# Six buffers in place of three for the tiles named `lt` in a hybrid attention and RWKV-7 decoder layer

## The chip, the cores and the metric

The kernel runs on one core of a Trainium2 chip. The metric is the device time of one execution in microseconds. A core has five engines that work side by side, each through its own instructions in a fixed order, and wait for each other by semaphores: PE (matmuls, and transposes done as matmuls), DVE (vector work), ACT (activations and copies), POOL (elementwise work and fills) and SP (here it only issues DMAs). PEld in a profile is PE's loading of weights.

## The reference, cut to what matters

One decoder layer on a sequence of 1024 tokens of width 1024: a dilated window attention and an RWKV-7 time mixing side by side, merged by gates, and then a squared-ReLU MLP. The change lies in the RWKV-7 part, which is a recurrence over the tokens for 16 heads of 64 channels:

```python
def step(state, inp):
    r_t, w_t, k_t, v_t, a_t, b_t = inp
    sa = jnp.einsum('bhvk,bhk->bhv', state, a_t)
    state = (state * w_t[:, :, None, :] + sa[..., None] * b_t[:, :, None, :]
             + v_t[..., None] * k_t[:, :, None, :])
    return state, jnp.einsum('bhvk,bhk->bhv', state, r_t)
...
y = wkv7_scan(rh, wh, kh, vh, -kk, kk * ah)
mu = jnp.mean(y, axis=-1, keepdims=True)
var = jnp.mean(jnp.square(y - mu), axis=-1, keepdims=True)
y = ((y - mu) * lax.rsqrt(var + GN_EPS)).reshape(B, S, C) * gn_w + gn_b
```

## The kernel before, in words

The heads are handled in 8 pairs (m = 0 to 7; the text calls them pair 0 to pair 7), since two heads fill the 128 partitions. The tokens are cut into 16 chunks of 64, and inside a chunk the recurrence becomes a triangular system. For each pair these steps are written down, in the order of the string `ORDER` (a letter for the step, a digit for the pair):

- P and G: projections, which are dense matmuls on PE at L307 (G are the 16 gate projections, of which one is written per pair and the rest at the end). They need nothing of the recurrence and fill PE between the steps below.
- E and F: the small projections and the features of the pair (L694 to L709 on DVE). L709 writes the second operand of the next step, in two halves.
- g: the products inside the chunks (PE L749), which DVE takes out of PSUM with a mask (L755 into `lm`, L757 into `fe`).
- I, the inverse: DVE L769 transposes `lm` into `lb`; 30 dependent steps of two instructions (L775, L777) on DVE solve the unit triangular systems with `lb` and a scratch area in `tt`; L781 transposes the result into `tt`. From L769 to the end of L781 is called the solve below. PE transposes further operands meanwhile (L785, L722).
- L, the local part: block-diagonal operands `bd` are filled by copies (`place`, L805), from `tt` for the first and the third of them. PE transposes parts of `lm` (L816) and `ar` (L820) into PSUM, ACT copies these into two tiles `xx` (L817, L822). Then come six groups of four matmuls (L838), each of a `bd` with an `xx`, their results (L840, L843, L845), and 8 groups of four matmuls (L853) that finish `fe` (L854, L855, L858).
- C, the chain: 16 dependent steps over the chunks, in each a matmul of each head (PE L874) and its scaling (DVE L877). ACT copies the result into `y` (L880).
- N, the norm: squares of `y` into `sq` (L888), their sum (DVE L890), a reciprocal root in small DVE instructions (L137 to L142), its product with `y` (POOL L894), transposes on PE (L900), ACT L904, POOL L908, DVE L912, and a DMA out of `sq`.

The tiles are given out from pools, and a scheduler, when the kernel is built, sets the fixed order of each engine's instructions: it takes the written order as priority, and an instruction gets its place once its operands and a free buffer are there by the scheduler's own reckoning. So the number of buffers decides both which tile an instruction waits for on the chip, and where it stands in its engine's queue. Matmul results go to PSUM tiles named `s`, of which there are two buffers.

Six tiles of 4 KB per partition are taken under the one name `lt` for each pair, in this order:

```python
lb = f4.tile([64, 32, 32], F32, name="lt", bufs=NLT)
tt = f4.tile([64, 32, 32], F32, name="lt", bufs=NLT)
xx = [f4.tile([128, 2, 4, 128], F32, name="lt", bufs=NLT) for h in range(2)]
y = f4.tile([128, 16, 64], F32, name="lt", bufs=NLT)
sq = f4.tile([128, 16, 64], F32, name="lt", bufs=NLT)
```

With three buffers in turn, `lb` and the second `xx` share one, `tt` and `y` share one, and the first `xx` and `sq` share one. So L817 into the second `xx` waits until L781 has read `lb`.

Of the kernel before, what the change touches and what calls it, by code (L numbers as in the profile page):

```python
# [30 lines left out]
OGR = ((0, 1), (2, 3), (4,), (5,), (6,), (7,))  # L31
OPV = 0
OQ = 0
NBD, NFT, NLT, NW, NGT, NRK = 5, 6, 3, 4, 2, 4
NGA, NAD = 1, 7
NAP, NSA = 4, 3
DVE_K, PE_K, POOL_S, NAT, NX0 = (0, 2, 3, 5), (1, 4, 6, 7), (1, 3), 6, 4
# [1374 lines left out]
```

## Time and profile before

| | us |
|---|---|
| median of three runs (2270.26 to 2278.08) | 2275.87 |
| the profiled execution, its own time | 2280.91 |
| span of that execution, first to last instruction | 2279.2 |
| PE busy in the span (10002 instructions) | 2090.6 (92%) |
| DVE busy | 1567.8 (69%) |
| ACT busy | 1036.3 (45%) |
| POOL busy | 621.9 (27%) |

Busy time is the time in which an engine had an instruction of the program running. PE's matmuls overlap, so that a busy PE is not PE at its peak. The granted clock of PE is either full (1.00) or half (0.50) at any time; its mean over this execution is 0.961. The solves of the eight pairs run from 503 us to 1279 us of the span, one about every 106 us.

### The profile page before, as it was taken

What the parts mean: (1) busy time and instruction counts of PE and PEld (TensorE: products, weight loads), DVE (VectorE), ACT (ScalarE), POOL (GpSimd) and SP (SyncE); (2) the same over time, 40 slices, a digit from 0 to 9 for tenths busy, and PEclk for the clock granted to TensorE, in tenths of its full rate; (3) what the DMA queues carried; (4) which work ended last, traced back from release to release, by engine and by line L of the source; (5) the groups of instructions that cost most, each with busy time, mean ns of one, the idle gap of its engine ahead of it and who ended that gap; (6) DMA issues with size and microseconds to landing.
All of it is one profiled execution on the core that took longest, in us unless ns stands there. A gap on an engine that the chain in (4) does not pass through costs nothing. (4 is left out here: it accounts for less than half of the span.)

```text
span 2279.2 us, 28241 instructions
## 1 busy us (share of the span) xinstructions
PE 2090.6 (92%) x10002; PEld 1628.6 (71%) x10002; DVE 1567.8 (69%) x2845; ACT 1036.3 (45%) x2018; POOL 621.9 (27%) x461
## 2 busy tenths in 40 slices
PE   6798999988989989898989999998699999999997
PEld 3676676666777767677777778876467777788876
DVE  5845555468879787867877744428766553799997
ACT  5534433345454635444645442126545443533332
POOL 2504310321213131222222133201000000988860
PEclk9999999999999999998998999999899999999998
DMA  7513311100011110101010164323354333433222
GB/s 257 169 31 102 98 38 33 56 28 24 25 33 37 31 34 29 34 29 34 24 48 31 54 202 144 125 93 118 118 168 161 116 106 125 155 128 114 93 102 74
DMA packets 156315, 194.88 MB, mean 86 GB/s; under 512 B 10729, under 2 KB 110211, under 8 KB 154127
## 3 DMA queue, kind: packets, MB, share of 16 engines
q1 hardware_dynamic: 156175, 193.08, 25.5%
q8 instruction: 79, 1.29, 0.2%
q14 instruction: 61, 0.50, 0.1%
HBM read 152.14 MB, written 40.90 MB: 85 GB/s over the span
## 5 line engine op out<-in xcount | busy, mean ns | idle before, releaser
L307 PE MATMUL d<-hh,w_h 128*128 128x512 f32 x960 | 329.0, 415 | 7.2 <-ACT w_h L64 4.0
L307 PE MATMUL d<-hl,w_h 128*128 128x512 f32 x960 | 331.1, 415 | 2.9 <-DVE hl L280 2.9
L307 PE MATMUL d<-hh,w_l 128*128 128x512 f32 x960 | 324.8, 410 | 2.6 <-DVE w_l L65 2.6
L1108 PE MATMUL m<-op 128*128 128x512 f32 x1272 | 295.8, 394 | 11.5 <-POOL op L65 6.4
L65 POOL TENSOR_TENSOR w_l<-w_t,w_h 128x256 fp32r<-128x256 f32 x160 | 129.3, 810 | 633.6 <-PE d L307 293.4
L1108 PEld LDWEIGHTS m<-op 128*128 128x128 f32 x1272 | 240.0, 190 | 66.9 <-POOL op L65 10.6
L1108 PE MATMUL m<-big,op 128*128 128x512 f32 x1152 | 275.1, 399 | 5.1 <-ACT op L64 2.1
L1108 PEld LDWEIGHTS m<-big,op 128*128 128x128 f32 x1152 | 212.8, 188 | 67.3 <-DVE u L1220 4.2
L64 ACT CAST w_h<-w_t 128x256 fp32r<-128x256 f32 x272 | 108.7, 404 | 316.4 <-PE d L307 230.7
L307 PEld LDWEIGHTS d<-hl,w_h 128*128 128x128 f32 x960 | 181.5, 193 | 45.5 <-issue 10.1
L307 PEld LDWEIGHTS d<-hh,w_h 128*128 128x128 f32 x960 | 180.8, 193 | 46.3 <-issue 5.7
L307 PEld LDWEIGHTS d<-hh,w_l 128*128 128x128 f32 x960 | 181.1, 192 | 44.0 <-issue 8.5
L64 ACT CAST op<-t 128x512 fp32r<-128x512 f32 (+1 forms) x152 | 114.2, 776 | 182.8 <-PE m L1108 121.5
L65 DVE TENSOR_TENSOR op<-t,op 128x512 fp32r<-128x512 f32 (+1 forms) x124 | 118.5, 975 | 28.0 <-ACT op L64 27.8
L153 POOL TENSOR_TENSOR macc<-macc,ada_t 128x512 f32<-128x512 f32 x56 | 87.5, 1564 | 181.3 <-ACT macc L151 162.7
L1266 POOL TENSOR_TENSOR t<-big 128x1024 f32<-128x1024 f32 x7 | 16.9, 2410 | 352.1 <-DMA big<-in_w_ff_dram 331.3
L1282 DVE TENSOR_TENSOR big<-big,m 128x1024 f32<-128x1024 f32 x88 | 104.4, 1210 | 3.8 <-PE m L1108 3.8
L775 DVE TENSOR_TENSOR lt<-lt 64x30 f32<-64x30 f32 (+14 forms) x240 | 96.9, 404 | 8.2
L777 DVE TENSOR_TENSOR lt<-lt 64x30 f32<-64x30 f32 (+14 forms) x240 | 94.2, 392 | 7.7
L874 PEld LDWEIGHTS ch<-sv,fe 128*128 128x128 f32 x512 | 83.3, 191 | 20.3 <-DVE sv L877 8.9
L65 DVE TENSOR_TENSOR w_l<-w_t,w_h 128x256 fp32r<-128x256 f32 x112 | 61.6, 555 | 48.6 <-ACT w_h L64 34.9
L65 POOL TENSOR_TENSOR op<-t,op 128x1024 fp32r<-128x1024 f32 x28 | 93.2, 3339 | 4.3 <-ACT op L64 4.3
(379 smaller groups left out, 3925.8 us busy)
## 6 DMA issues: line engine op xcount, KB each, us to landing
w_t<-in_w_in_dram SPq DMA_DIRECT2D x240, 128.0 KB
ada_t<-in_ada_w_dram SPq DMA_DIRECT2D x64, 256.0 KB
fS<-ft SPq DMA_DIRECT2D x64, 256.0 KB
t<-in_w_ff_dram SPq DMA_DIRECT2D x16, 1024.0 KB
big<-fS SPq DMA_DIRECT2D x16, 1024.0 KB
big<-in_w_ff_dram SPq DMA_DIRECT2D x16, 1024.0 KB
x<-in_x_dram SPq DMA_DIRECT2D x16, 512.0 KB
ada_t<-in_ada_w_dram SPq DMA_DIRECT2D x16, 512.0 KB
```

The costliest lines, as they stand in the source:

```text
L64: nc.scalar.copy(hi, t)
L65: (eng or nc.vector).tensor_tensor(lo, t, hi.bitcast(F32), OP.subtract)
L153: nc.gpsimd.tensor_tensor(acc, acc, t, OP.add)
L307: nc.tensor.matmul(p[:, 512 * half + cs.start:512 * half + cs.stop], a, b[half][k][:, cs], start=k == ks[0] and i == 0, stop=k == ks[-1] a ...
L775: nc.vector.tensor_tensor(q, lb[:, s + 1:32, s:s + 1].to_broadcast([64, n, s]), lb[:, s:s + 1, 0:s].to_broadcast([64, n, s]), OP.mult)
L777: nc.vector.tensor_tensor(lb[:, s + 1:32, 0:s], lb[:, s + 1:32, 0:s], q, OP.add)
L874: nc.tensor.matmul(ps[h][:, c8, :], fe[b][:, h, c8, :], sv[h][b][:, c8, :], start=True, stop=True)
L1108: self.nc.tensor.matmul(p, s, m, start=start and k == 0 and i == 0, stop=k == len(a) - 1 and i == 2, skip_group_check=not start)
L1266: vb.tensor_tensor(sb[:, 0], wr[:, k1, h2], wr[:, k1, h1], OP.subtract)
L1282: nc.vector.tensor_tensor(acc[nm][h], acc[nm][h], ps2[h], OP.add)
```

## The change

One constant becomes 6, so that each of the six tiles of a pair has a buffer of its own, which it shares only with the tile of the same role of the next pair:

```diff
-NBD, NFT, NLT, NW, NGT, NRK = 5, 6, 3, 4, 2, 4
+NBD, NFT, NLT, NW, NGT, NRK = 5, 6, 6, 4, 2, 4
```

No instruction is added or removed. The order of the instructions changes from the local part of pair 0 to the start of the merge; ahead of that and behind it it is the same. Three places follow.

On PE, between the end of pair 3's early transposes and its first L838, before the change (`b_6579` is `lm` of pair 3; `bd_3719` and `bd_3717` are the first operands of its two heads; rows of L307 are left out at the cut):

```order
L816 MATMUL s<-ident,b_6579 128x128 x4
L307 MATMUL d<-hh,w_h 128x512
L816 MATMUL s<-ident,b_6579 128x128 x4
L820 MATMUL s<-ident,ar 128x128 x4
...
L307 MATMUL d<-hh,w_l 128x512 x2
L816 MATMUL s<-ident,b_6579 128x128 x8
L820 MATMUL s<-ident,ar 128x128 x4
L838 MATMUL s<-lt,bd_3719 128x128 x4
L307 MATMUL d<-hh,w_h 128x512 x2
L838 MATMUL s<-lt,bd_3717 128x128 x4
```

The same place in the changed kernel:

```order
L816 MATMUL s<-ident,b_6579 128x128 x4
L820 MATMUL s<-ident,ar 128x128 x4
L816 MATMUL s<-ident,b_6579 128x128 x4
L307 MATMUL d<-hl,w_h 128x512 x2
L816 MATMUL s<-ident,b_6579 128x128 x4
L820 MATMUL s<-ident,ar 128x128 x4
...
L307 MATMUL d<-hh,w_l 128x512
L838 MATMUL s<-lt,bd_3719 128x128 x4
L838 MATMUL s<-lt,bd_3717 128x128 x4
```

The second eight L816 and four L820 have moved from behind the long run of L307 to ahead of it, and L838 is now the first instruction of pair 3 behind that run. It is so in pairs 1 to 7, where the run itself has between 68 and 85 L307 in place of 74 to 88; in pair 0 all sixteen L816 stay behind the run, as before. In pairs 5 and 7, seven of the eight groups of L853 stand ahead of the chain's first L874, where four did before.

On DVE, at the end of pair 3's chain and the start of its norm, which pair 4's products (L755 and L757, `b_7453` is `lm` of pair 4) are woven into, before the change (`b_7360` is an operand of pair 4 that the features write):

```order
L705 TENSOR_TENSOR b_7360<-rkv,ft 128x8x64
L877 TENSOR_SCALAR sv<-ch_7292,dd 64x64
L877 TENSOR_SCALAR sv<-ch_7291,dd 64x64
L707 COPY dd<-ft 64x8 x2
L708 TENSOR_TENSOR ar<-ft 128x2x256
L877 TENSOR_SCALAR sv<-ch_7292,dd 64x64
L709 TENSOR_TENSOR ar<-rkv,ft 128x2x256
L755 TENSOR_TENSOR b_7453<-s,gmask 128x4x2x32
L757 TENSOR_TENSOR fe<-s,gmask 128x4x64
L755 TENSOR_TENSOR b_7453<-s,gmask 128x4x2x32
L757 TENSOR_TENSOR fe<-s,gmask 128x4x64
L890 TENSOR_REDUCE va<-lt 128x16
```

The same place in the changed kernel:

```order
L877 TENSOR_SCALAR sv<-ch_7292,dd 64x64
L704 SCALAR_TENSOR_TENSOR b_7360<-ft 128x8x64
L705 TENSOR_TENSOR b_7360<-rkv,ft 128x8x64
L707 COPY dd<-ft 64x8 x2
L708 TENSOR_TENSOR ar<-ft 128x2x256
L709 TENSOR_TENSOR ar<-rkv,ft 128x2x256
L890 TENSOR_REDUCE va<-lt 128x16
L755 TENSOR_TENSOR b_7453<-s,gmask 128x4x2x32
L891 TENSOR_SCALAR va<-va 128x16
L757 TENSOR_TENSOR fe<-s,gmask 128x4x64
L137 TENSOR_SCALAR rsg_r<-va 128x16
L755 TENSOR_TENSOR b_7453<-s,gmask 128x4x2x32
```

The last L877 of the chain now stands ahead of five feature instructions that stood among the chain's steps, and the first two pairs of L755 and L757 have moved behind L890. Pair 6 has the same order as pair 4, and pair 2 nearly the same. Before the change, pairs 3, 5 and 7 already had L890 ahead of all their L755, and still do.

On PE, at the same point: pair 4's last products, and pair 3's transposes of the norm (`b_7360` as above), before the change:

```order
L749 MATMUL s<-ar,b_7360 128x128 x8
L307 MATMUL d<-hl,w_h 128x512
L785 MATMUL s<-ident,b_7360 128x128 x4
L307 MATMUL d<-hl,w_h 128x512
L900 MATMUL ch_7427<-ident,lt 128x128 x4
L900 MATMUL ch_7436<-ident,lt 128x128 x4
```

The same place in the changed kernel:

```order
L749 MATMUL s<-ar,b_7360 128x128 x8
L307 MATMUL d<-hh,w_h 128x512
L749 MATMUL s<-ar,b_7360 128x128 x5
L900 MATMUL ch_7427<-ident,lt 128x128 x4
L900 MATMUL ch_7436<-ident,lt 128x128 x4
L749 MATMUL s<-ar,b_7360 128x128 x3
L785 MATMUL s<-ident,b_7360 128x128 x4
```

Pair 4's last products now stand behind the norm's transposes of pair 3. It is so for pairs 2, 4 and 6; for pairs 3, 5 and 7 it was so before the change and is so after it.

## Rows read from the trace of the kernel before

**Rows 1.** Windows view, solve's end to next solve's start: engines' busy time, PEclk, DMA, GB/s.
```profile
538.50:605.90 67.40, 64.32 (x353) 52.68 (x353) 49.28 (x121) 35.23 (x69) 10.73 (x12) 0.86 0.05 15
645.70:705.30 59.60, 56.38 (x349) 46.58 (x350) 47.41 (x119) 34.42 (x64) 10.90 (x14) 0.97 0.08 25
742.60:816.20 73.60, 68.75 (x385) 55.69 (x385) 52.03 (x122) 37.01 (x67) 14.70 (x17) 0.91 0.09 28
854.10:915.30 61.20, 58.09 (x356) 47.39 (x356) 48.35 (x120) 34.73 (x65) 11.62 (x15) 0.97 0.09 27
953.80:1031.80 78.00, 73.42 (x386) 60.18 (x387) 51.59 (x122) 38.51 (x71) 14.88 (x17) 0.85 0.09 26
1069.90:1131.80 61.90, 58.90 (x356) 48.67 (x356) 48.23 (x118) 34.88 (x65) 11.50 (x15) 0.95 0.08 26
1169.60:1243.00 73.40, 68.89 (x381) 56.90 (x381) 50.54 (x121) 38.15 (x72) 14.18 (x16) 0.87 0.10 33
```

**Rows 2.** Waits of PE from 490 to 1345 us: total, times, longest.
```profile
PE s L816 <- ACT lt L817: 37.6, 8, 6.2
```

**Rows 3.** Timeline of PE behind pair 3's solve: start, duration, idle before it.
```profile
854.65 1.97 PE L816 MATMUL s<-ident,b 128*128 128x128 f32 x8 [5.24 <-ACT lt L817]
...
857.26 1.22 PE L838 MATMUL s<-lt,bd 128*128 128x128 f32 x8
```

**Rows 4.** Timeline of DVE at the same place.
```profile
850.31 3.83 DVE L781 STREAM_TRANSPOSE lt<-lt 32x1024 f32<-32x1024 f32 x2
854.16 1.82 DVE L805 COPY bd<-lt 32x128 f32<-32x128 f32 x6
858.51 0.45 DVE L805 COPY bd<-lt 32x128 f32<-32x128 f32 x2 [2.53 <-PE s L838]
```

**Rows 5.** Timeline of PE behind pair 4's solve, at half clock.
```profile
957.38 1.91 PE L838 MATMUL s<-lt,bd 128*128 128x128 f32 x8
```

**Rows 6.** Timeline of DVE ahead of pair 4's solve.
```profile
903.44 0.29 DVE L877 TENSOR_SCALAR sv<-ch,dd 64x64 f32<-64x64 f32 x1
...
915.26 4.00 DVE L769 STREAM_TRANSPOSE lt<-b 32x1024 f32<-32x1024 f32 x2
```

**Rows 7.** Timeline of DVE ahead of pair 3's solve.
```profile
790.42 0.55 DVE L877 TENSOR_SCALAR sv<-ch,dd 64x64 f32<-64x64 f32 x2
...
796.20 0.35 DVE L707 COPY dd<-ft 64x8 f32<-64x8 f32 x2
...
798.97 1.21 DVE L890 TENSOR_REDUCE va<-lt 128x16 f32<-128x1024 f32 x1
...
816.16 1.97 DVE L769 STREAM_TRANSPOSE lt<-b 32x1024 f32<-32x1024 f32 x1
```

**Rows 8.** Timeline of PE in that stretch.
```profile
797.78 0.62 PE L307 MATMUL d<-hl,w_h 128*128 128x512 f32 x2
798.24 0.61 PE L307 MATMUL d<-hh,w_l 128*128 128x512 f32 x2
...
801.59 1.13 PE L749 MATMUL s<-ar,b 64*128 64x128 f32 x8 [2.51 <-DVE fe L757]
```

**Rows 9.** Windows view: pair 3's chain, then tails ahead of pairs 4, 3, 5.
```profile
874.70:904.20 29.50, 28.68 (x180) 23.38 (x179) 26.98 (x67) 15.70 (x26) 4.54 (x6) 1.00 0.06 15
903.40:915.30 11.90, 11.56 (x77) 9.25 (x75) 10.74 (x34) 4.48 (x9) 5.61 (x6) 1.00 0.08 23
790.40:816.20 25.80, 22.34 (x121) 17.57 (x119) 19.33 (x46) 7.69 (x13) 9.63 (x10) 0.87 0.07 21
1001.00:1031.80 30.80, 27.33 (x123) 21.81 (x123) 19.84 (x46) 8.89 (x16) 10.11 (x10) 0.72 0.06 18
```

**Rows 10.** Timeline in pair 4's solve: POOL's last sum of the norm and DVE.
```profile
921.81 2.51 POOL L908 TENSOR_TENSOR lt<-lt,rkv 128x1024 f32<-128x1024 f32 x1 [5.48 <-ACT lt L904]
922.13 2.36 DVE L775 TENSOR_TENSOR lt<-lt 64x150 f32<-64x150 f32 x1
```

**Rows 11.** Timeline of PE in pair 1's local part: one group of L853 at full clock.
```profile
665.50 1.05 PE L853 MATMUL s<-fe,b 128*128 128x128 f32 x8
```

## The prediction

> **What bounds the kernel now.** I read the page first: PE is busy 92% of the span, and the change touches only the RWKV-7 part, about 490 to 1340 us. There I split the time by pairs with the windows view. A solve keeps DVE busy and takes about 38 us, as from the L769 at 816.16 to the end of L781 at 854.14 [rows 4, 7]. The change adds nothing to it. What differs is the stretch from one solve's end to the next one's start: 59.6, 61.2 and 61.9 us ahead of pairs 2, 4 and 6, but 73.6, 78.0 and 73.4 us ahead of pairs 3, 5 and 7 [rows 1]. In these stretches no engine is alone the bound: PE is busy for 56 to 73 us of them and DVE for 47 to 52, and they hand results to each other. So the reader should see a loop over the pairs (solve, local part, chain, products of the next pair, solve), in which a step that comes earlier brings all later steps forward. PE's projections (L307) fill its gaps in that loop; since the changed order leaves only 7 more of them behind the last solve, I count the time of the loop, not PE's work, which stays the same.
>
> Then I read PE's waits. The largest is in front of L816: 37.6 us in 8 waits, one for each pair [rows 2]. The timeline shows its cause: in pair 3 PE is idle for 5.24 us, until L817 can write the second `xx`, which is free only when L781 has read `lb` [rows 3, 4]. After that come eight L816 (1.97 us), four L820, and L838 at 857.26, which is 3.1 us after the solve's end at 854.14.
>
> **The change part by part.** No instruction comes or goes; buffers and order change.
>
> *The wait at L816.* With a buffer of its own, `xx` is filled before the solve ends, and PE meets the solve only at L838, whose `bd` is copied from `tt`. DVE's six copies took 1.82 us, 0.30 each [rows 4]; two of them belong to the first head, so L838 can start some 0.7 us behind the solve instead of 3.1: 2.4 us earlier. In pairs 0, 4 and 6 the first L838 came 3.6 us behind, as in pair 4, where it stands at 957.38 [rows 5] and the solve ended at 953.8 [rows 1]: 2.9 us. Five times 2.4 and three times 2.9 make 20.7 us. DVE gains with it, since its L805 waited 2.53 us for that L838 [rows 4]. The wait itself doesn't go: PE still runs out of projections before the solve ends, and the moved transposes cover only a part. So the granted clock, which is at the lower of its two levels (1.2 GHz in place of 2.4) behind this wait, will now be low under L838: eight of them took 1.91 us at half clock [rows 5] and 1.22 us where the clock recovered under them [rows 3]. I take 0.7 us off for each pair, 5.5 in all. This term is a gain of 15.2 us, between 13.7 (only 2.4 in each pair, and the 0.7 lost) and 20.7 (nothing lost).
>
> *The rule that promises more.* The Trainium skill's page "Perfetto Trace Analysis", section "Optimization Strategy", says that the same gap coming back on the engine that should be busy can mean that there are too few buffers for the next tile. By it the gap would close, and the sum for this term would be 37.6 us. The trace agrees on the cause, L817's wait for the buffer [rows 2], but not on the price, since L838 needs the same solve.
>
> *The tails ahead of pairs 2, 4 and 6.* Here the changed order speaks against the change. Before, the last chain step of pair 3 (L877) ended at 903.73 on DVE and the solve of pair 4 began at 915.26, 11.5 us later [rows 6]. Pair 3's own tail was of the other kind: from the last L877, which ended at 790.97, to L769 at 816.16 it took 25.2 us [rows 7], since DVE first finished the features, then took L890, and only then cleared PSUM with L755 and L757, while PE stood idle for 2.51 us [rows 8] and then ran at a low clock (0.87 of full in the mean, 0.72 ahead of pair 5 [rows 9]). In the changed order pairs 2, 4 and 6 get that kind. Their tail is then: L704, L705, L707, L708 and L709, 2.8 us (796.20 to 798.97), and from L890 to L769 17.2 us (798.97 to 816.16) [rows 7]: 20.0 us, so 8.5 us more than 11.5. Three things lessen it. The features that moved leave the chain shorter by up to 2.8 us if DVE sets the chain's pace, and by nothing if PE does; pair 3's chain had PE busy 28.7 of 29.5 us and DVE 27.0 [rows 9], nearly alike, and I take 1.9. The norm now comes ahead of the solve by more, so POOL's L908 may lie less beside the solve's instructions, of which one took 2.36 us next to it [rows 10], against about 0.3 for its neighbours: 0 to 2.0, I take 1. And PE's wait ahead of the second L749 is shorter here: 19 projections stand ahead of it behind the chain, 4.4 us at 0.23 us each (797.78 to 798.24 for two [rows 8]), against 2.8 us of features and the 2.6 us from L890 to the second L749 (798.97 to 801.59) [rows 7, 8], so it is about 1.0 us in place of 2.51. The low clock in the tail ahead of pair 3 cost 3.4 us (a mean of 0.87 over 25.8 us is 6.7 us at half speed, of which half is lost); I take half of it away, 1.7. That leaves 8.5 - 1.9 - 1.0 - 1.7 = 3.9 us for each, 11.7 us for the three. The bounds for one are 0.3 us (8.5 - 2.8 - 2.0 - 3.4) and 13.5 us (8.5 and the 5.0 by which the tail ahead of pair 5 was longer than that ahead of pair 3 [rows 9]).
>
> *The clock, by the skill.* The Trainium skill's page "TensorE: Matmul & The Clock Gate", section "HAM oscillation — how this bites in real kernels", says that a wait which returns in each round of a loop makes the clock fall anew each time, and that half of the throttled time is lost. The 3.4 us above are worked out in that way; rows 9 show the fallen clock in two of the three tails that have the wait and a full one where it is missing.
>
> *The chains of pairs 4 and 6.* In the local parts that follow the solves of pairs 5 and 7, and by the same order in both, three more groups of L853 stand ahead of the first L874. At 1.05 us for a group [rows 11] this delays a chain by 0 (they had to run anyway) to 3.2 us; I take 1 for each, 2 in all.
>
> *The tails ahead of pairs 3, 5 and 7* keep their order: 0, or a gain of up to 5.0 if the one ahead of pair 5 takes the shorter time of pair 3's. The first stretch hardly changes in order. The bonus, the DMA out of `sq` and the start of the merge lie beside PE's projections and cost nothing; without that cover the bonus alone would be L908's 2.5 us [rows 10]. The 7 projections left for the end cost 1.6 us at 0.23 each.
>
> **The sum**: -15.2 + 11.7 + 2 + 1.6 = +0.1 us. The profiled execution took 2280.9 us, so 2281.0; it is 5.0 us over the median of the runs shown, so 2276 us as a median. That is no change: a measurement of this kernel tells about 0.3%, 6.8 us, from nothing.
>
> **The rivals.** *Slower, the tails decide*: the low clock stays in all three new tails and nothing is given back in the chain, so 8.5 to 11 us for each, 25 to 33 in all, with 2 to 6 for the chains of pairs 4 and 6 and 1.6 for the end, against 15: +14 to +26, about 2293. For it: the wait of 2.51 us and a low clock behind it came with each of the tails of that kind: the stretches ahead of pairs 3, 5 and 7 have a mean clock of 0.85 to 0.91, the others but the first 0.95 to 0.97 [rows 1]. It decides from about 6 us for each tail. Against it: PE's wait there is shorter. *Faster, the order of the tails costs little*: DVE sets the pace of the chain and the clock holds, so about 1 us for each tail, and most of the gain of 15 to 20 us stays: about -13 us, 2263. For it: the same work is done, only later, and the longest tail (pair 5) can hardly get worse. *The gap closes*, as the page on traces has it: -37.6 + 11.7 + 3.6, about 2254. Against it stands L838's need of `tt`. That the change doesn't do what it says I leave out, since the moved L816 show that the buffers are free.
>
> **Chances.** No change (within 0.3%) 0.38; slower by the tails 0.31; faster 0.31, of which 0.04 for the closed gap. The likeliest case alone would lie between 2269 and 2283. The range leaves out the closed gap and the ends where all bounds fall together: 16 us below 2276 to 20 us above it, 2260 to 2296.
>
> **What would show it.** Right: PE's wait at L816 is gone, and a wait of about 3 to 4 us stands at L838 in each pair, with L838 some 0.7 us behind the end of L781; DVE's wait ahead of the second L805 is gone; the stretches ahead of pairs 2, 4 and 6 are 2 us longer than before and those ahead of 3, 5 and 7 some 2 us shorter. Wrong: all stretches shrink (faster), or those ahead of pairs 2, 4 and 6 take over 68 us with a granted clock below 0.9 (slower), or the first L838 is held by something else than L805.

## The result, and the profile after

The changed kernel takes 2301.3 us (2290.6 to 2306.8, median of 4 runs) beside 2275.9 us (2270.3 to 2278.1) of the kernel before on the same chip: a ratio of 1.011 with a 95% interval of 1.0068 to 1.0151. It is 25 us slower, and 5 us outside the predicted range. Its profiled execution took 2299.8 us, with a span of 2298.0 us and a mean granted clock of 0.954, where the kernel before had 0.961. Two of the kernels below each had one execution with a mean granted clock under 0.7 (2740 and 2868 us), which is left out of their medians.

The windows view from one solve's end to the next one's start, which answers to [rows 1]:

```profile
538.20:602.70 64.50, 59.76 (x345) 48.53 (x346) 50.23 (x119) 33.08 (x61) 10.16 (x11) 0.92 0.05 13
642.40:712.30 69.90, 65.34 (x353) 52.37 (x353) 49.12 (x119) 33.57 (x59) 13.38 (x16) 0.89 0.08 24
748.50:825.20 76.70, 71.16 (x373) 57.72 (x373) 52.02 (x122) 35.00 (x62) 14.71 (x17) 0.86 0.09 27
863.60:931.50 67.90, 62.90 (x358) 50.62 (x359) 50.53 (x121) 33.68 (x60) 13.10 (x15) 0.93 0.09 26
967.90:1040.90 73.00, 67.57 (x376) 53.42 (x377) 51.67 (x122) 34.74 (x62) 15.11 (x17) 0.93 0.09 28
1079.00:1150.50 71.50, 66.01 (x353) 53.54 (x353) 50.16 (x119) 34.52 (x61) 12.89 (x15) 0.86 0.07 23
1186.70:1261.30 74.60, 70.35 (x373) 56.64 (x373) 50.68 (x121) 35.55 (x65) 14.41 (x16) 0.87 0.10 33
```

Ahead of pairs 2, 4 and 6 the stretch grew by 10.3, 6.7 and 9.6 us, to 69.9, 67.9 and 71.5. The other four changed by -2.9, +3.1, -5.0 and +1.2 us. The seven make +23.0 us; the solves became 2.6 us shorter in sum. Pair 7's solve ends at 1298.8 us in place of 1278.7, and behind that nothing more is lost: the whole loss arises in the loop over the pairs.

PE's waits from 490 to 1365 us (total, times, longest), to be set beside [rows 2]:

```profile
PE s L838 <- ACT bd L805: 19.8, 4, 5.5
PE s L838 <- DVE bd L805: 16.2, 3, 6.0
PE s L749 <- DVE fe L757: 10.6, 8, 2.6
```

The wait at L816 is gone, and 36.0 us in place of its 37.6 stand at L838, as forecast, though 5.1 us in each of seven pairs where the forecast had 3 to 4. The timelines of PE and of DVE behind pair 3's solve answer to [rows 3] and [rows 4], and the last row is the chain's last L877, which answers to the first of [rows 6]:

```profile
864.21 3.75 PE L838 MATMUL s<-lt,bd 128*128 128x128 f32 x16 [5.14 <-ACT bd L805]
```
```profile
859.76 3.81 DVE L781 STREAM_TRANSPOSE lt<-lt 32x1024 f32<-32x1024 f32 x2
863.60 1.42 DVE L805 COPY bd<-lt 32x128 f32<-32x128 f32 x6
...
866.29 0.45 DVE L805 COPY bd<-lt 32x128 f32<-32x128 f32 x2 [0.64 <-PE s L838]
...
912.72 0.29 DVE L877 TENSOR_SCALAR sv<-ch,dd 64x64 f32<-64x64 f32 x1
```

L838 comes 0.6 us behind the solve's end at 863.6 in place of 3.1. But the chain ends 49.4 us behind it (913.01), where it ended 49.6 us behind it before (903.73 from 854.1): the gain didn't reach the end of the chain. Over pairs 1 to 6 the last L874 ended 49.6 us behind the solve in the mean before, and 50.1 now.

The tail ahead of pair 4, PE and then DVE:

```profile
918.41 1.13 PE L749 MATMUL s<-ar,b 64*128 64x128 f32 x8 [0.16 <-DVE fe L757]
920.49 1.44 PE L749 MATMUL s<-ar,b 64*128 64x128 f32 x8 [0.95 <-DVE fe L757]
921.86 1.22 PE L307 MATMUL d<-hh,w_h 128*128 128x512 f32 x2
922.88 1.05 PE L307 MATMUL d<-hl,w_h 128*128 128x512 f32 x2
923.73 1.01 PE L307 MATMUL d<-hh,w_l 128*128 128x512 f32 x2
924.67 1.71 PE L749 MATMUL s<-ar,b 64*128 64x128 f32 x16
...
928.82 1.09 PE L900 MATMUL ch<-ident,lt 128*128 128x128 f32 x8 [0.77 <-POOL lt L894]
929.84 0.93 PE L749 MATMUL s<-ar,b 64*128 64x128 f32 x6
```
```profile
915.32 0.68 DVE L709 TENSOR_TENSOR ar<-rkv,ft 128x512 f32<-128x512 f32 x1
915.92 1.21 DVE L890 TENSOR_REDUCE va<-lt 128x16 f32<-128x1024 f32 x1
917.16 0.42 DVE L755 TENSOR_TENSOR b<-s,gmask 128x256 f32<-128x256 f32 x1
...
925.86 0.42 DVE L755 TENSOR_TENSOR b<-s,gmask 128x256 f32<-128x256 f32 x1 [1.89 <-PE s L749]
...
930.81 0.42 DVE L755 TENSOR_TENSOR b<-s,gmask 128x256 f32<-128x256 f32 x1 [2.04 <-PE s L749]
...
931.48 1.97 DVE L769 STREAM_TRANSPOSE lt<-b 32x1024 f32<-32x1024 f32 x1
```

Behind the wait of 0.95 us PE's clock falls: two L307 take 1.22 us there, and 0.62 at full clock [rows 8]. Six of them and, further on, the eight L900 of the norm stand between the last L749, and DVE, which clears their PSUM, waits for PE.

### The profile page after: what moved, and what is told of

It is laid out like the page before. It is cut to its first block, busy times and chain, and to the rows that moved or that the text cites. A ratio compares the mean times of both kernels' runs of the same rounds, so it can differ in the third digit from the quotient of the medians.

```text
span 2298.0 us, 28194 instructions
## 1 busy us (share of the span) xinstructions
PE 2107.5 (92%) x10002; PEld 1636.0 (71%) x10002; DVE 1563.3 (68%) x2845; ACT 1037.2 (45%) x2018; POOL 623.7 (27%) x461
## 5 line engine op out<-in xcount | busy, mean ns | idle before, releaser
L307 PE MATMUL d<-hh,w_h 128*128 128x512 f32 x960 | 330.2, 416 | 7.3 <-ACT w_h L64 4.0
L307 PE MATMUL d<-hh,w_l 128*128 128x512 f32 x960 | 327.2, 414 | 3.6 <-DVE w_l L65 3.6
L307 PE MATMUL d<-hl,w_h 128*128 128x512 f32 x960 | 329.3, 414 | 0.0
L1108 PEld LDWEIGHTS m<-op 128*128 128x128 f32 x1272 | 239.1, 189 | 66.5 <-POOL op L65 10.4
L307 PEld LDWEIGHTS d<-hh,w_h 128*128 128x128 f32 x960 | 182.4, 195 | 47.1 <-issue 6.2
L307 PEld LDWEIGHTS d<-hh,w_l 128*128 128x128 f32 x960 | 182.0, 194 | 44.8 <-issue 7.4
L307 PEld LDWEIGHTS d<-hl,w_h 128*128 128x128 f32 x960 | 183.2, 194 | 41.5 <-issue 8.6
L874 PEld LDWEIGHTS ch<-sv,fe 128*128 128x128 f32 x512 | 82.0, 192 | 28.7 <-DVE sv L877 16.9
L838 PE MATMUL s<-lt,bd 128*128 128x128 f32 x384 | 62.5, 328 | 36.1 <-ACT bd L805 19.8
```

The costliest lines, as they stand in the source:

```text
L307: nc.tensor.matmul(p[:, 512 * half + cs.start:512 * half + cs.stop], a, b[half][k][:, cs], start=k == ks[0] and i == 0, stop=k == ks[-1] a ...
L838: nc.tensor.matmul(p[:, g, :], bds[h][i][:, g, :], x[i // 2][:, g, :], start=True, stop=True)
L874: nc.tensor.matmul(ps[h][:, c8, :], fe[b][:, h, c8, :], sv[h][b][:, c8, :], start=True, stop=True)
L1108: self.nc.tensor.matmul(p, s, m, start=start and k == 0 and i == 0, stop=k == len(a) - 1 and i == 2, skip_group_check=not start)
```

## Experiments

From here on a stretch is named by the pair ahead of whose solve it lies. Times are medians, ratios are against the kernel before on the same chip (its medians were 2274.3 to 2276.9 us), each with its 95% interval.

**Buffers or order.** The first two kernels have six buffers, but each engine's instructions are chained to the order of a table (edges of order on the engine alone, without a semaphore):

```diff
-NBD, NFT, NLT, NW, NGT, NRK = 5, 6, 3, 4, 2, 4
+NBD, NFT, NLT, NW, NGT, NRK = 5, 6, 6, 4, 2, 4
...
+        for a, b in zip(row, row[1:]):
+            tc.add_manual_dep(at[b], a, mybir.DependencyInfo(mybir.DependencyClass.NoSync, mybir.DependencyReason.DATA),
```

> Six buffers as in the changed kernel, but every engine's row pinned to the order that the kernel before had. Theory ORDER (the loss comes from the rows that the scheduler chose once buffers were free, not from the buffers): within 0.3% of the kernel before, 2270 to 2283 us. The wait of PE at L816 stays for the greater part (at least 25 of 37.6 us), since on ACT the copies out of these transposes stand behind copies that need the solve. Rival BUFFERS (the six buffers, or their place in memory, cost by themselves): 2290 to 2305 us with the stretches ahead of pairs 2, 4 and 6 at 68 to 72 us.

2279.9 us, 1.0019 (0.9999 to 1.0040): no change that could be told. The wait at L816 was 28.6 us in 7. So the six buffers by themselves make at most 9 of the 25 us (the upper end of the interval), and no cost of theirs could be told.

> As the run before it, and for pairs 1 to 7 the second half of the transposes on PE and their copies on ACT moved to directly behind the first half, ahead of the long run of L307; nothing else moves. Theory ORDER: L838 starts 0.6 to 1.1 us behind the end of the solve in place of 3.1 to 3.6; the time lies between 2261 (the predicted gain of 15.2 us reaches the end of the chain) and 2276 us (it is lost within the chain, as the ends of the chain in the changed kernel suggest: 49.1 us behind the solve, 49.2 before); I take 2272. Rival WAIT (taking the wait away costs by itself, by half clock under L838 or by work that collides): 2285 us or more.

2276.8 us, 1.0016 (0.9993 to 1.0038). In pairs 1 to 7 L838 came 0.6 to 1.0 us behind the solve, but the solves grew by 6 us in sum: the moved rows push PE's projections back, and within the solve DVE's L543 waited for one (9.5 us in 9 from 490 to 1330 us, 7.5 of them in six solves; 0.9 us in 2 before). One such row of its timeline of DVE:

```profile
1042.35 1.28 DVE L543 SCALAR_TENSOR_TENSOR rkv<-d,col,rkv 128x1023 f32<-128x1023 f32 x1 [1.21 <-ACT rkv L542]
```

**The wait alone.** This kernel moves the same rows less far, as here in pair 4:

```diff
  L816 x4, L307, L816 x4, L820 x4
- L307 x75, L816 x8, L307, L820 x4
+ L307 x67, L816 x4, L307 x2, L816 x4, L820 x4, L307 x7
  L838 x4
```

> Six buffers, the rows of the kernel before; the second half of the transposes stands ahead of only the last eight L307 of the run, their copies ahead of the copies that need the solve. In the run with these rows ahead of the whole run the wait at L816 was gone, L838 came 0.6 to 1.0 us behind the solve, but DVE's L543 within the solve waited up to 1.8 us for its product and the solves grew by 6 us in sum; here it shouldn't wait. If that was where the gain went: 2262 to 2270 us. If the gain is lost because PE has the same work to do and only its pause moves (PE BOUND): 2272 to 2280 us.

2263.4 us, 0.996 (0.9943 to 0.9977): faster than both kernels. In pairs 1 to 7 L838 comes 0.6 to 1.1 us behind the solve, the chain ends 48.1 us behind it in the mean, and the waits around the solve's end are 20.5 us in 7 (two rows of PE's waits from 490 to 1330 us), with L543 as before the change:

```profile
PE s L838 <- DVE bd L805: 15.5, 5, 4.5
...
PE s L838 <- ACT bd L805: 5.0, 2, 2.7
```

A second run with the same rows on PE and DVE, meant as a control for a run further on:

> Control for the run with the features later: the rows of the run that moved the wait alone, with PE and DVE pinned and ACT, POOL and SyncE left to the scheduler. All theories: as that run, 2258 to 2270 us.

2273.0 us, 0.9993 (0.9978 to 1.0008), which was not expected. On ACT copies out of the moved transposes (L817, L822) had gone back behind those that need the solve (L805), and PE waited for them again. From this run, two rows of the timeline of ACT behind pair 3's solve, and one of PE's waits from 490 to 1330 us:

```profile
855.34 0.62 ACT L805 COPY bd<-lt 32x128 f32<-32x128 f32 x2 [5.91 <-DVE lt L781]
855.98 0.37 ACT L817 COPY lt<-s 128x256 f32<-128x256 f32 x1
```
```profile
PE s L820 <- ACT lt L817: 28.4, 7, 4.4
```

So L838 came 1.7 to 3.4 us behind the solve, and the gain was gone. The same rows on PE and DVE, with the wait at L838 and with it at L820, are 10 us apart by the medians and 7 by the ratios. The moved wait is the largest difference of the two and not the only one: other rows of ACT and four of POOL changed place too.

**Which buffers.** With own buffers for `xx` alone (`name="xx", bufs=2`), and with `NLT = 4`, the scheduler is free:

> Only the operands of the triangular solve get two buffers of their own; the inverse's input and output, chain and norm go on sharing three; the scheduler is free. Theory ORDER: the rows again come out with the lora products behind the first groups of L853 in the chain of every second pair, so 2285 to 2305 us, with three stretches over 67 us that were about 60. Rival CHAIN BUFFERS (the own buffers of y and sq make the loss): 2268 to 2283 us.

2290.0 us, 1.0075 (1.0047 to 1.0102): ORDER is right in the sign and at the lower end of its range; the stretches ahead of pairs 4 and 6, 61.2 and 61.9 us before, are now 73.0 each, two where three were expected.

> Four buffers in place of three or six; the scheduler is free. PE's rows then alternate from pair to pair as in the changed kernel, shifted by a pair: the lora products stand behind three groups of L853 in chains 1, 3 and 5, and behind six in chains 2, 4 and 6. LATE FEATURES: the first L749 at 44 to 46 us and 49 to 51 us behind the solve, as in the changed kernel, 2288 to 2306 us. Rival (the fifth and sixth buffer cost by themselves): 2268 to 2283 us.

2304.7 us, 1.0128 (1.0098 to 1.0158). The loss is there with four buffers, and the fifth and sixth add nothing that could be told.

**Which rows.** In the next four runs the scheduler is free again, and the table of steps or the priority of some steps is changed. The first writes `"... F2 g2 I2 N1 V2 ..."` in place of `"... F2 N1 g2 I2 V2 ..."`:

> The changed kernel with the norm of the pair before written behind the next pair's products and inverse in the table of steps, so that L890, L900 and L911 leave the tail; the scheduler is free. If the norm in the tail makes the loss: the stretches ahead of pairs 2, 4 and 6 fall from 69.9, 67.9 and 71.5 to 60 to 65 us and the time to 2260 to 2280 us. If the late lora products and features make it: the first L749 stays 44 to 46 us behind the solve, these stretches lose the 2 to 4 us of the norm alone, and the time is 2285 to 2297 us.

2324.4 us, 1.0213 (1.0178 to 1.0247), above both ranges. The norm left the tail, and the seven stretches sum to 480 us in place of the 498 of the changed kernel. But the solves, in which DVE now has the norm's L890 and its small instructions, take 285 us in place of 262, and in the order that came out the features are later too: ahead of pairs 2 to 7 the first L749 came 47 to 56 us behind the solve. So a tail without the norm isn't enough.

> The changed kernel with the lora step written ahead of the local part in the table of steps, so that L645 to L653 stand under the solve, before L838; features, chain and norm keep their order. LATE FEATURES through late lora products: the first L749 comes 40 us or less behind the solve, and the time is 2262 to 2285 us. If it isn't the lora products but the place of L683 and of the features' rows on DVE and ACT between the chain's steps that sets the features, the first L749 stays at 44 us or later and the time is 2288 us or more.

2283.9 us, 1.0042 (1.0023 to 1.0062), the best of the free orders. The time lies in the first range, but its sign did not come: ahead of pairs 3, 4, 6 and 7 the first L749 still came 45 to 46 us behind the solve. The seven stretches sum to 459 us, less than the 475 before, but the solves to 280 in place of 265, in which DVE now has rows of the lora step too (E, the small projections): what the stretch gains the solve gives back.

> The changed kernel with a higher priority in the scheduler for the next pair's lora products and features; nothing else. Its PE rows then have eight of the 32 L749 in the middle of the chain and most of the others between its last L874. If late features make the loss (theory LATE FEATURES): the first L749 comes 36 us or less behind the solve in every stretch, the stretches ahead of pairs 2, 4 and 6 fall from 69.9, 67.9 and 71.5 to 62 us or less, and the time is below that of the changed kernel by at least 15 us, 2255 to 2285 us. Rival CHAIN (the features' work on DVE and ACT between the chain's steps costs as much as it saves): the last L874 ends 54 us or more behind the solve in place of 49, and the time is 2285 to 2310 us.

2362.4 us, 1.0376 (1.0343 to 1.0408), slower than both had it. In the chains of pairs 1 to 6 the last L874 ended 62 to 76 us behind the solve.

> The same priority in the kernel before, with three buffers. LATE FEATURES: its long stretches (73.6, 78.0 and 73.4 us ahead of pairs 3, 5 and 7), where the first L749 came at 49 to 51 us, fall to 65 us or less, 2240 to 2268 us. CHAIN: the chain ends 54 us or more behind the solve, and the time is 2270 to 2295 us.

2389.0 us, 1.0506 (1.0469 to 1.0542); the chain ended 67 to 71 us behind the solve there. CHAIN is right in the sign, and the loss is far larger than it had: with the features' work among its steps the chain takes longer.

Next, the tails' rows on PE. Into the changed order's tails (all six), and into three of the order before:

> Six buffers and the rows of the changed kernel on every engine, but in the tails ahead of pairs 2 to 7 PE's eight L900 stand behind the last L749, and between groups of eight L749 stands one L307, the others (5 to 10 a tail) ahead of the second half of the products. TAIL ROWS (what stands between the last L749, run at half clock, makes the stretches long): the six tails shorten by 2 to 4 us each, 2277 to 2289 us. Rival CLOCK (the pauses and the half clock stay, or the L307 put ahead delay the products by as much): 2295 to 2306 us.

2295.2 us, 1.0091 (1.0068 to 1.0114): not to be told from the changed kernel. But the tails did shorten. The six stretches took 64.5, 69.8, 65.6, 71.2, 68.5 and 71.0 us, 15 us less in sum than in the last run of this study, which has the changed kernel's order, and the solves took 14 us more. With L900 behind the products the norm ends later, and DVE's L912 waits for it within the solve (1.2 us in 2 in the changed kernel). From DVE's waits from 490 to 1365 us:

```profile
DVE lt L912 <- POOL lt L908: 18.4, 6, 3.4
```

> Six buffers, the rows of the kernel before, but in the tails ahead of pairs 3, 5 and 7 PE's L900 behind the last L749, and the six L307 between the last groups moved ahead of the group before (into the pause of 2.5 us that stood there). TAIL ROWS: these three stretches shorten by 3 to 6 us each, 2260 to 2270 us, and the half clock behind that pause goes or gets shorter. CLOCK: the spell of half clock stays and eats it, 2274 to 2282 us.

2273.5 us, 0.9979 (0.9959 to 0.9998). The three stretches were 70.9, 69.7 and 70.9 us in place of 73.6, 78.0 and 73.4, the solves behind them 2.5 us longer each, by the same wait of L912 (9.4 us in 3; none before). Half clock behind the pause stayed, 10 to 14 us long.

> The edits of the two runs before it together. If both gains hold and add, 2250 to 2262 us, faster than both kernels; PE BOUND or CLOCK: 2268 to 2280 us.

2263.4 us, 0.996 (0.9941 to 0.9978): no more than the wait alone.

Then one thing at a time between the slow and the fast order, first the features' place:

> The rows of the run that moved the wait alone (six buffers, 2263 us), PE and DVE pinned, the other engines left to the scheduler; in chains 1, 3 and 5 the next pair's features (L694 to L709 on DVE) stand six chain steps later, so that 22 or 23 L877 stand ahead of the first L709 as in the changed kernel, in place of 16 or 17, and the first L749 on PE six L874 later. FEATURES' PLACE: the stretches ahead of pairs 2, 4 and 6 grow from 57, 61 and 61 us by 5 to 10 us each, 2280 to 2295 us. Rival (the place of the features is hidden by the other work of the tail, the loss is made elsewhere): 2258 to 2270 us.

2292.5 us, 1.0082 (1.0064 to 1.0100), and stretches of 66.2, 73.1 and 73.7 us where the control had 59.1, 60.4 and 60.4. But the chain itself ended 55 to 62 us behind the solve; in the changed kernel the chains ahead of pairs 4 and 6 end at 50. PE's L749 stand among its last steps and waited for the features for 1.2, 0.4 and 0.1 us; the larger part is half clock (PEclk 0.90, 0.88 and 0.76 from the first to the last L874, 1.00 in the control). So it costs more than what it was to copy.

> The rows of the changed kernel, PE and DVE pinned; in chains 1, 3 and 5 the lora products and the features of pairs 2, 4 and 6 are put back to the place among the steps of local part and chain that the kernel before gave them (16 or 17 L877 ahead of the first L709). FEATURES' PLACE: the stretches ahead of pairs 2, 4 and 6 fall from 69.9, 67.9 and 71.5 to 60 to 65 us, 2275 to 2288 us. Rival (the rows of the tail, or the half clock, make the loss): 2294 to 2306 us.

2312.7 us, 1.0159 (1.0124 to 1.0193). The first L749 came at 41 to 43 us in place of 45 to 46, but the chains ended at 53 to 55, and the stretches stayed at 69 to 72. It isn't told whether the features' place or the stalled chain did it.

Last, the tails again, with the changed kernel as a control beside them:

> The rows of the run that moved the wait alone (six buffers, 2263 us), but in the tails ahead of pairs 2, 4 and 6 PE's rows as in the changed kernel: 19 L307 ahead of the first eight L749, 6 ahead of the next eight, one ahead of the last, and the eight L900 ahead of the last three L749 (before: 5 or 6, 5 or 10, 1 to 6, and L900 behind). Chain and features are not touched. TAIL ROWS: the stretches ahead of 2, 4 and 6 grow from 57, 61 and 61 us by 5 to 9 us each, the time to 2277 to 2290 us. Rival (DVE sets the tail and PE's rows are hidden): 2260 to 2270 us.

2287.2 us, 1.0049 (1.0032 to 1.0066): 24 us more than without those tails by the medians, 20 by the ratios. The stretches ahead of pairs 2, 4 and 6 are 64.8, 66.6 and 66.5 us, where the windows view of the run with the wait alone gave 57.0, 61.0 and 61.3; DVE's busy time (the third) is the same to 0.12 us. This run, and behind it the one with the wait alone:

```profile
647.80:712.60 64.80, 58.40 (x351) 47.87 (x352) 47.45 (x119) 33.59 (x62) 13.15 (x15) 0.97 0.08 25
...
862.10:928.70 66.60, 60.89 (x357) 49.95 (x358) 48.32 (x120) 33.47 (x60) 12.77 (x15) 0.94 0.08 25
```
```profile
641.10:698.10 57.00, 53.45 (x337) 43.71 (x338) 47.33 (x118) 32.95 (x60) 11.02 (x14) 1.00 0.08 26
...
845.30:906.30 61.00, 57.45 (x344) 47.12 (x344) 48.32 (x120) 33.07 (x59) 11.69 (x15) 0.95 0.09 27
```

Two waits for POOL, which the changed kernel has not at that length, make a part of it: L900 waits 2.8, 2.4 and 2.4 us in the three tails (0.77 us above), and L912 9.4 us in 3 in the solves behind them. The row of L900 in the timeline of PE ahead of pair 4:

```profile
925.41 1.09 PE L900 MATMUL ch<-ident,lt 128*128 128x128 f32 x8 [2.42 <-POOL lt L894]
```

> The changed kernel with PE and DVE pinned, and in the tails ahead of pairs 2, 4 and 6 PE's L307 and L900 put behind the last L749 but for five ahead of each of the first two groups and one ahead of the last. Chain and features are not touched. TAIL ROWS: these stretches fall from 69.9, 67.9 and 71.5 to 61 to 65 us, the time to 2278 to 2288 us. Rival (the features that come 2 to 6 us later, and DVE): the stretches fall by less than 2 us, 2294 to 2306 us.

2322.6 us, 1.0204 (1.0187 to 1.0222): slower by 23 us where the theory had it faster. Without the projections PE has nothing to do until the features are there. Two rows of its timeline of PE ahead of pair 4:

```profile
922.64 3.83 PE L749 MATMUL s<-ar,b 64*128 64x128 f32 x16 [3.53 <-DVE fe L757]
...
931.13 3.07 PE L749 MATMUL s<-ar,b 64*128 64x128 f32 x16 [2.23 <-DVE rsg_t L140]
```

Sixteen take 3.83 us here, at the lower level of the clock, beside 1.71 in the rows above. The stretches were 69.4, 70.9 and 71.0 us, beside 66.8, 67.9 and 67.3 in the control. The edit made two new waits. In the tails DVE's L543 waited for its projection, 4.3, 4.5 and 4.5 us. And since L900 now stands behind the moved projections, the norm was waited for in the solve: L912 stood 8.3, 7.8 and 7.7 us there, and these three solves took 43 to 44 us in place of 36. Two rows of the timeline of DVE, the first in the tail ahead of pair 4 and the second in its solve:

```profile
928.87 1.28 DVE L543 SCALAR_TENSOR_TENSOR rkv<-d,col,rkv 128x1023 f32<-128x1023 f32 x1 [4.50 <-ACT rkv L542]
...
951.18 1.29 DVE L912 TENSOR_TENSOR lt<-lt,ch 128x512 f32<-128x512 f32 x2 [7.82 <-POOL lt L908]
```

So this run doesn't decide on the theory.

> Control: the changed kernel with the rows of PE and DVE pinned to what they are, so that nothing moves; timed beside the two other runs on the same chip. All theories: 2293 to 2307 us.

2299.2 us, 1.0094 (1.0068 to 1.0120), as the changed kernel. With the first run it is the cleanest pair of the study: the same six buffers and instructions, 2279.9 us in the one order and 2299.2 in the other (19 us; 17 by the ratios).

## Why the prediction was wrong

The account that holds all runs together is that of the loop from the end of pair 0's solve to the end of pair 7's, by the windows view: before, after, with the wait alone, and in the last run, whose order is that of the changed kernel (span, then the busy time of PE, and further on PEclk).

```profile
538.50:1278.70 740.20, 669.48 (x3574) 533.32 (x3574) 596.57 (x1327) 379.54 (x784) 165.82 (x198) 0.93 0.11 33
```
```profile
538.20:1298.80 760.60, 684.05 (x3575) 538.93 (x3575) 600.61 (x1327) 379.47 (x781) 167.58 (x197) 0.92 0.10 32
```
```profile
536.90:1260.10 723.20, 657.33 (x3578) 519.06 (x3578) 599.80 (x1327) 378.63 (x782) 165.66 (x198) 0.95 0.11 34
```
```profile
545.10:1297.00 751.90, 673.14 (x3575) 530.10 (x3575) 599.40 (x1326) 379.19 (x781) 168.62 (x197) 0.93 0.10 32
```

PE runs nearly the same instructions in all of them (3574 to 3578) and is busy for nine tenths of the loop. In the first three it is idle for 70.7, 76.6 and 65.9 us (span less busy time), and the rest of the difference in span, 14.6 and 12.2 us, is busy time, which grows or shrinks as the granted clock falls or rises: half clock cost 51, 63 and 33 us of the three loops (the span times what the mean granted clock, unrounded, lacks of 1). How the loss is split differs from one execution to the next. In the fourth, with the same order as the second, PE is idle for 78.8 us, 8.1 more than before, and busy for only 3.6 more at the same PEclk of 0.93. The prediction said that in these stretches no engine is alone the bound, and summed steps that come earlier or later. A sum of that kind must be checked against PE: a step that comes earlier helps only if PE is idle for less, or at half clock for less.

*The wait at L816 (-15.2 us): the gain did not reach the end of the chain, the larger of the two errors.* Its mechanism is right: the wait moved to L838, which came 0.6 to 1.1 us behind the solve but in pair 0, and DVE's wait ahead of the second L805 fell from 2.53 to 0.64 us. With the other rows left where they were it is worth 7 to 10 us (the run with the wait alone beside the second run with its rows on PE and DVE). In the changed kernel the gain was lost within the chain, which ended as late as before: up to the last L874 the seven stretches took 3.7 us more in sum than before (0.4 less in the last run), where the forecast had 13.2 less (-15.2 + 2). The step that failed is "a step that comes earlier brings all later steps forward": PE's idle time in the loop did not fall with the wait.

*The tails ahead of pairs 2, 4 and 6 (+11.7 us): mis-sized, by 11 us.* The base of 8.5 us for each was nearly right: from the last L874 to L769 these tails took 10.4, 11.0 and 11.0 us before and 16.2, 17.6 and 21.2 now, 7.6 us more in the mean and 22.7 in sum (19.2 in the last run). The 4.6 us that I took off were not given back. The chain wasn't shorter: the first L709 stands behind 22 or 23 L877 in place of 16 or 17, and the chain's end stayed (pairs 3 and 5) or came 4.5 us later (pair 1, with a PEclk of 0.87 from its first to its last L874, where it was 1.00 before). The pause ahead of the second L749 is short, 0.95 us as worked out (1.0), but a fall of the clock follows it all the same: in the tails ahead of pairs 4 and 6 PE was at half clock for 3.4 and 17.1 us behind it (3.4 in both in the last run). And the sum had no term for PE's rows between the later L749: six L307 and the L900, for which DVE then waits. DVE's waits for L749 went from the first row (before) to the second (after), in the waits view of DVE from 490 to 1345 us:

```profile
DVE b L755 <- PE s L749: 32.9, 22, 3.9
```
```profile
DVE b L755 <- PE s L749: 44.2, 23, 3.7
```

*The chains of pairs 4 and 6 (+2) and the end (+1.6)* cost nothing. The seven groups of L853 ahead of the first L874 stand in pairs 4 and 6, not in pairs 5 and 7 as the prediction and the part ahead of it have it: in the trace 56 of their 64 L853 come first, 32 before, and in pairs 5 and 7 24 both times. Pair 4's and pair 6's first L874 came some 2 us later, but their chains ended as before. Behind the loop the changed kernel took 999.2 us, and 1000.5 before.

*The tails ahead of pairs 3, 5 and 7 (0 to -5.0)*: the stretch ahead of pair 5 became shorter by 5.0 us, as its bound said, the other two longer by 3.1 and 1.2.

Of the rivals, "slower, the tails decide" came true with its sign of failure (over 68 us with a clock below 0.9 ahead of pairs 2 and 6, 67.9 and 0.93 ahead of pair 4) and a price of +14 to +26 against the 25 measured; its point of decision, 6 us for each tail, was passed in all three (6.8, 6.9 and 10.5 us from the last L877 to L769). That its price fits is in part luck: it kept 15 us of gain from the wait, which did not come, and gave the three tails 25 to 33 us, where they took 22.7. "The gap closes", drawn from the Trainium skill's page "Perfetto Trace Analysis", section "Optimization Strategy", did not happen: the wait only changed its place.

What the runs settle: neither the buffers nor the moved wait makes the loss, but the order that the scheduler chose once it had them. Rows of that order in the tails are enough for a loss of 20 to 24 us in the fast order, part of it by waits of L900 and L912 that the changed kernel has not at that length. Taking them out of the changed order did not give the loss back: the tails got 15 us shorter in one run, and the solves 14 us longer by the wait for the norm. What they leave open is the share of each row, and of the features that come later: both runs that moved these also made the chain longer. Moving the ACT and PE rows of features and chain together was not tried.

## What to carry to other kernels

Where a scheduler places the instructions, a change of a pool's buffers is a change of the program's order, and most of its effect can lie far from the wait that it removes; pin the order and the edit can be timed alone (here 9 us faster in place of 25 slower). A wait that moves to the next instruction on the same engine is a gain only by what the engine's idle time and half clock lose together, so count both over the whole loop. Work that fills a gap is itself needed by a time: projections moved behind the products were waited for in the tail (L543), and the norm moved behind them in the next solve (L912), so that a shorter tail came back as a longer solve. Time the whole loop, not the stretch that was edited.

## What was not expected of the hardware

A run's time follows its granted clock. In 99 runs of the kernel before, the mean clock lay between 0.956 (2285.6 us) and 0.966 (2264 to 2269 us), and a straight line through them falls by 1.7 us for each 0.001; the runs scatter about it by some 3 us. By that line the whole gain of the run with the wait alone (median clock 0.967 against 0.961) is one of the clock, and 7 to 10 us of the changed kernel's loss are (0.955 and 0.957 in its two sets of runs). The line doesn't tell what makes the clock fall.

The clock doesn't fall behind each pause. In the windows of 10 us around the ends of the solves of pairs 1 to 4, with the wait alone, it was full behind pauses of 0.91, 2.3 and 2.7 us, and 0.66 behind one of 4.5 us (pair 3):

```profile
640.10:650.10 10.00, 8.10 (x48) 6.17 (x47) 9.40 (x19) 8.74 (x20) 1.52 (x3) 1.00 0.23 79
734.70:744.70 10.00, 6.76 (x41) 5.77 (x42) 9.63 (x19) 4.78 (x11) 1.45 (x2) 1.00 0.12 35
844.30:854.30 10.00, 7.94 (x37) 7.25 (x37) 8.28 (x17) 4.96 (x12) 1.45 (x2) 0.66 0.06 16
943.10:953.10 10.00, 7.01 (x42) 6.02 (x43) 9.63 (x19) 5.03 (x13) 1.46 (x2) 1.00 0.14 41
```

In the tails ahead of pairs 3, 5 and 7 a pause of 2.5 us ahead of L749, always at the same place, was followed by half clock for 6.8, 20.5 and 17.1 us in the kernel before, and for 20.5, 6.8 and 20.5 us in the changed kernel. Ahead of pairs 4 and 6 of the changed kernel it fell behind the 0.95 us told of above. So the length of the pause alone doesn't tell.
